# An encoder layer with neighbourhood attention: queries and keys reach their operands by four token tiles instead of by two

## The chip, the core and the metric

The kernel runs on one core of one Trainium2 chip. The metric is the device time in microseconds (us) of one execution. Below, TensorE (PE) is the matrix engine, VectorE (DVE) and ScalarE (ACT) the two engines that read and write both kinds of on-chip memory, GpSimd (POOL) a slower one that cannot reach PSUM, and SyncE (SP) issues all of the DMAs.

## What is computed

One layer is applied to two sequences, a sample of 1024 tokens (8 tiles of 128) and a prompt of 512 tokens (4 tiles). Cut to what matters:

```python
h = rms_norm(x, norm_g)
u_pool, g_pool, q, k, v, g_attn = split(h @ w_in)      # each 512 wide
pool_out = pool_mixer(u_pool, w_pool, pool_scale) * silu(g_pool)
q = rms_norm(q.reshape(B, S, 8, 64), q_norm_g) * 64 ** -0.5
k = rms_norm(k.reshape(B, S, 8, 64), k_norm_g)
attn_out = neighbourhood_attention(q, k, v, rpb) * silu(g_attn)
y = x + concatenate([pool_out, attn_out]) @ w_out
```

The attention sees the tokens as rows of 64 columns; a query sees 8 rows by 16 columns of keys. The 8 heads are worked on in 4 pairs.

## The kernel before, in words

Every matrix product is made of three float32r products, high by high, high by low and low by high, where "low" is what is left of a float32 number after its high part. The helper `split` makes both parts, `low` the second one.

The program goes through the four head pairs of the sample, then through the four of the prompt, then through the output projection (tiles `acco`). For each pair `project_qkv` multiplies a token tile of 128 tokens by 384 columns (queries, keys and values of two heads) into a PSUM bank `acc_s` or `acc_p`: 24 matmuls of 128x384 a tile. For the first pair of the sample four tiles are interleaved; for the others one tile follows another, and the last two are interleaved. Then `gate` and `u_block` make three (prompt) or six (sample) blocks of 24 matmuls of 128x512 (`accg`, `accu`), `attention` makes scores `s`, transposes `pt` and products `po`, and `pooling` the other branch.

What the change touches lies in `project_qkv`. ScalarE copies a finished tile to SBUF (`qkv`, a ring of `QBUFS` = 4 buffers). The squares of its queries and keys (`s2`) are summed per head into `st4`. After two tiles VectorE scales the sums (one `tensor_scalar`) and `rsqrt` takes the reciprocal root of all of them in 11 small instructions. VectorE then multiplies the queries and keys of each tile by these factors, and TensorE transposes them, four 128x128 transposes into one PSUM bank `ptq` (tag `pt`, of which there are two; the attention's transposes take the same tag). From that bank ScalarE writes, for each head of the pair, the keys twice and the queries once (64 partitions by 256), and VectorE writes the low parts of keys and queries. The values go by `vd` in DRAM to the tiles `v`, four loads for two token tiles.

Two engines never work on one PSUM bank at once: the planner makes any access to a bank wait for the accesses that other engines recorded on it before. So in the bank `ptq` all six copies of ScalarE come first, and the four of VectorE after them.

The order on each engine is not the order of the code. Every call is recorded as an operation of `Plan`, with its needs; `Plan.order` then runs a list schedule with costs written by hand and emits the operations in the order that it finds. Matmuls of the projections and blocks have the priority `MAIN` and stay in the order of the program; scores, transposes and attention products have an earlier priority and slip in between as soon as they are ready in the plan. An operation on TensorE counts as ready `TO_PE` = 800 ns after what it needs has ended on another engine. Loading and splitting of weights has the first priority (`FIRST`). On the chip each engine then runs its list strictly in order.

Of the kernel before, what the change touches and what calls it, by code (L numbers as in the profile page):

```python
# [14 lines left out]
F32 = mybir.dt.float32  # L15
# [323 lines left out]
def encoder(ctx, tc, xn_p, xt_p, xn_s, xt_s, w_in, w_out, w_pool, pscale, ng, qg, kg,  # L339
# [26 lines left out]
    qk_t = sb.tile([P, 2], F32, name="qk_t")  # L366
    gqk = sb.tile([P, 1], F32, name="gqk")
# [125 lines left out]
    class Sequence:  # L493
# [63 lines left out]
        def project_qkv(self, p, w, group=1):  # L557
# [3 lines left out]
            for t0 in range(0, self.NT, 2):  # L561
                st4 = ring("st4", 2, [P, 4, 8], f"st4_{sq}_{p}_{t0}")
                qkvs = []
                for t in (t0, t0 + 1):
# [28 lines left out]
                rsqrt(st4[:, 2], st4[:, 3], st4[:, 1])  # L593
                pt = bank("pt", f"ptq_{sq}_{p}_{t0}")
                for i, t in enumerate((t0, t0 + 1)):
                    qkv = qkvs[i]
                    vt = ring("vt", 2, [P, 2, 2, HD], f"vt_{sq}_{p}_{t}", F32R)
                    split(vt[:, :, 0], vt[:, :, 1], qkv[:, 256:384].rearrange("p (h d) -> p h d", d=HD))
                    sp.dma_start(out=vd[t * P:(t + 1) * P, :], in_=vt.rearrange("p h s d -> p (h s d)").bitcast(F32))
                    qn = qkv[:, 0:256].rearrange("p (h d) -> p h d", d=HD)  # L600
                    dve.tensor_tensor(out=qn, in0=qn, op=ALU.mult,
                                      in1=st4[:, 2, i * 4:i * 4 + 4].unsqueeze(2).to_broadcast([P, 4, HD]))
                    pe.transpose(pt[:, i * P:(i + 1) * P], in_=qkv[:, 0:P], identity=ident)
                    pe.transpose(pt[:, 256 + i * P:256 + (i + 1) * P], in_=qkv[:, P:256], identity=ident)
# [4 lines left out]
                rt, r0 = (2 * t0) // 8, (2 * t0) % 8  # L609
                lo, hi = 7 - r0, 3 - r0  # L610
                qa = slice(base + rt * 512, base + (rt + 1) * 512)
                ka = slice(base + t0 * P, base + t0 * P + 256)
                own = [slice(hd * HD, hd * HD + HD) for hd in range(2)]
                k_src = [pt[own[hd], 256:512] for hd in range(2)]
                q_src = [pt[own[hd], 0:256].rearrange("p (r cb c) -> p r cb c", r=4, cb=4) for hd in range(2)]
                q_dst = []
                for hd in range(2):
                    for rows in (own[hd], own[1 - hd]):
                        v = q[hd][rows, qa].rearrange("p (cb r c) -> p r cb c", cb=4, r=8)
                        q_dst.append(v[:, lo::-1, :, ::-1] if hi < 0 else v[:, lo:hi:-1, :, ::-1])  # L620
                for hd in range(2):
                    for rows in (own[hd], own[1 - hd]):
                        act.activation(out=k[hd][rows, ka], in_=k_src[hd], func=AF.Copy, scale=gqk[own[hd]])
                    act.activation(out=q_dst[2 * hd], in_=q_src[hd], func=AF.Copy)
                for hd in range(2):
                    low(k[2 + hd][own[hd], ka], k_src[hd], k[hd][own[hd], ka], gqk[own[hd]])
                    low(q_dst[2 * hd + 1], q_src[hd], q_dst[2 * hd])
                rg = t0 // 2
                for cb in range(4):
                    sa = bass.AP(vd.tensor, vd.offset + (rg * 4 * GW + C0[cb]) * 256,  # L630
                                 [[GW * 256, 4], [256, 32], [1, 256]])
                    sp.dma_start(out=vs[base // 256 + rg][:, cb].bitcast(F32), in_=sa)
# [126 lines left out]
    warm = sb.tile([P, 1], F32, name="warm")  # L759
    dve.memset(warm, 0.0)  # L760
    act.activation(out=warm, in_=warm, func=AF.Exp)
# [312 lines left out]
```

## Time and profile before

| | us |
|---|---|
| median of 3 runs | 648.9 (647.37 to 649.58) |
| the profiled execution | 648.4 |
| its span, first to last instruction | 646.6 |
| TensorE busy in the span | 635.0 |
| VectorE busy in the span | 557.1 |
| ScalarE busy in the span | 372.8 |
| GpSimd busy in the span | 100.6 |

The span is that of one profiled execution; 1.8 us of its time lie outside the span. Busy times are sums of what an engine's instructions took, so a busy TensorE still has to be looked at for how close its matmuls start to each other. The granted TensorE clock is 1.00 throughout.

### The profile page before, as it was taken

The page shows a single profiled execution, that of the slowest core. Times are in us where ns is not written, and L with a number is a line of the kernel's source. Part 1 is how long each engine was busy: PE and PEld are TensorE (multiplying, and loading weights), DVE is VectorE, ACT ScalarE, POOL GpSimd, SP SyncE. Part 2 cuts the span into 40 slices and gives each one's busy share as a digit, 9 for nine tenths or more (in the row PEclk, how much of TensorE's full clock was granted, in tenths as well). Part 3 has the DMA queues.
Part 4 walks back from the last instruction along what each step waited for, and adds up shares of the span by engine and source line. Part 5 has one row for each costly group of instructions (what it writes and reads, how often), then busy time and mean ns, then how long its engine had stood idle before and what let it go on. Part 6 is the DMA issues. An engine that isn't in the chain of part 4 may idle for free.

```text
span 646.6 us, 11390 instructions
## 1 busy us (share of the span) xinstructions
PE 635.0 (98%) x3404; PEld 567.0 (88%) x3404; DVE 557.1 (86%) x1647; ACT 372.8 (58%) x910; POOL 100.6 (16%) x142
## 2 busy tenths in 40 slices
PE   6999999999999999999999999999999999999997
PEld 5998899988899888999889989899899878887886
DVE  6688999899987999967999989989999989879742
ACT  5766786568656476544777556477566457323210
POOL 1130100000000000101001110021212423405412
PEclk9999999999999999999999999999999999999999
DMA  8974354442274522425344355545556687843631
GB/s 304 348 205 143 104 169 124 123 121 79 59 246 137 182 62 69 134 95 152 127 112 143 109 168 162 174 139 144 169 174 195 189 261 231 269 152 118 191 131 65
DMA packets 92961, 101.53 MB, mean 157 GB/s; under 512 B 12900, under 2 KB 78564, under 8 KB 92900
## 3 DMA queue, kind: packets, MB, share of 16 engines
q1 hardware_dynamic: 92900, 100.81, 50.7%
q8 instruction: 27, 0.44, 0.3%
q14 instruction: 34, 0.28, 0.1%
HBM read 81.41 MB, written 19.37 MB: 156 GB/s over the span
## 4 chain that ended last, share of the span: by engine, by line
PE 91%; DVE 4%; DMA 3%; issue 1%; ACT 0%; SPq 0%; DVEq 0%; ACTq 0%
PE acc_s L330 21%; PE acco L330 15%; PE accg_s L330 14%; PE acc_p L330 10%; PE accu_s L330 7%; PE accg_p L330 6%; PE po_s L330 4%; PE accu_p L330 3%; PE pt_s L330 3%; PE s_s L330 3%; DMA xr<-in_xn_s 1%; PE po_p L330 1%; PE ptq_s L330 1%; DVE B L330 1%; PE pt_p L330 1%
## 5 line engine op out<-in xcount | busy, mean ns | idle before, releaser
L330 PE MATMUL acc_s<-w_sA,ht_s 128*128 128x384 f32 x768 | 145.9, 342 | 6.3 <-DVE w_sA L330 6.3
L330 PEld LDWEIGHTS acc_s<-w_sA,ht_s 128*128 128x128 f32 x768 | 136.0, 190 | 7.6 <-ACT ht_s L330 5.9
L330 PE MATMUL accg_s<-ht_s,w_sT 128*128 128x512 f32 x384 | 100.4, 399 | 0.0
L330 PEld LDWEIGHTS accg_s<-ht_s,w_sT 128*128 128x128 f32 x384 | 70.0, 188 | 12.0
L330 PE MATMUL acc_p<-w_pA,ht_p 128*128 128x384 f32 x384 | 75.4, 339 | 0.7 <-DVE w_pA L330 0.5
L330 PEld LDWEIGHTS acc_p<-w_pA,ht_p 128*128 128x128 f32 x384 | 66.1, 188 | 1.8 <-DVE w_pA L330 0.8
L330 PE MATMUL acco<-B,left 128*128 128x512 f32 x228 | 56.2, 395 | 0.6 <-DVE left L330 0.6
L330 PE MATMUL accu_s<-ht_s,w_sT 128*128 128x512 f32 x192 | 53.0, 400 | 0.0
L330 PEld LDWEIGHTS acco<-B,left 128*128 128x128 f32 x228 | 41.9, 188 | 9.5 <-DVE left L330 1.0
L330 PE MATMUL accg_p<-ht_p,w_pT 128*128 128x512 f32 x192 | 47.6, 395 | 0.0
L330 PEld LDWEIGHTS accg_p<-ht_p,w_pT 128*128 128x128 f32 x192 | 35.3, 188 | 6.9
L330 ACT ACTIVATE k<-ptq_s,gqk 64x256 fp32r<-64x256 f32 x64 | 30.1, 470 | 18.8 <-PE ptq_s L330 18.1
L330 PEld LDWEIGHTS accu_s<-ht_s,w_sT 128*128 128x128 f32 x192 | 34.6, 188 | 5.1
L330 DVE TENSOR_TENSOR xr<-acco,xr 128x512 f32<-128x512 f32 x30 | 20.5, 686 | 20.4 <-PE acco L330 18.2
L330 ACT ACTIVATE ns_edge<-ns_edge,sm_s 128x288 f32<-128x288 f32 x54 | 28.4, 529 | 16.5 <-DVE sm_s L330 16.3
L330 ACT ACTIVATE ns_s<-ns_s,sm_s 128x384 f32<-128x384 f32 x53 | 31.7, 610 | 10.1 <-DVE sm_s L330 9.9
L330 DVE TENSOR_TENSOR pp_s<-pt_s,pp_s 128x384 fp32r<-128x384 f32 x64 | 34.5, 544 | 0.3
L330 PE MATMUL po_s<-pp_s,v 128*128 128x256 f32 x192 | 32.0, 287 | 0.0
L330 PE MATMUL s_s<-k,q 128*128 128x288 f32 (+1 forms) x128 | 31.4, 330 | 0.0
L330 PEld LDWEIGHTS po_s<-pp_s,v 128*128 128x128 f32 x192 | 28.9, 188 | 1.5
L330 POOL TENSOR_TENSOR vt_s<-qkv_s,vt_s 128x128 fp32r<-128x128 f32 x17 | 9.1, 540 | 122.0 <-ACT vt_s L330 97.3
L330 ACT ACTIVATE qkv_s<-acc_s,rr_s 128x384 f32<-128x384 f32 x24 | 13.7, 578 | 23.6 <-PE acc_s L330 20.9
(221 smaller groups left out, 1350.4 us busy)
## 6 DMA issues: line engine op xcount, KB each, us to landing
v<-vd_s SPq DMA_DIRECT2D x64, 128.0 KB
wr_sA<-in_w_in SPq DMA_DIRECT2D x32, 192.0 KB
wr_sT<-in_w_in SPq DMA_DIRECT2D x32, 192.0 KB
wr_pA<-in_w_in SPq DMA_DIRECT2D x32, 192.0 KB
wr_pT<-in_w_in SPq DMA_DIRECT2D x32, 192.0 KB
out<-xr SPq DMA_DIRECT2D x24, 256.0 KB
x<-in_xt_s SPq DMA_DIRECT2D x16, 256.0 KB
vd_s<-vt_s SPq DMA_DIRECT2D x32, 128.0 KB
```

The costliest lines, as they stand in the source:

```text
L330: op.fn()
```

## The change

A group of `project_qkv` is now four token tiles, not two. The sample has two groups a pair instead of four, the prompt one instead of two. `st4` holds 16 sums and factors in a row instead of 8, and uses its first part again for the helper values of `rsqrt`. The transposes of the queries go to one bank (`qt`), those of the keys to another (`kt`), both of the tag `pt`. Every copy out of them is 64 partitions by 512. Queries come first, and within a head the low part is recorded right behind its high part. The eight loads of values come behind. The factor `gqk` is now a column of the tile `qk_t`, and the tile `warm` is gone; its first activation works on `gqk`.

```diff
@@ -363,8 +363,8 @@
 
     g_sb = sb.tile([P, KC], F32, name="g_sb")
     ident = sb.tile([P, P], F32, name="ident")
-    qk_t = sb.tile([P, 2], F32, name="qk_t")
-    gqk = sb.tile([P, 1], F32, name="gqk")
+    qk_t = sb.tile([P, 3], F32, name="qk_t")
+    gqk = qk_t[:, 2:3]
     psc = sb.tile([P, NPAIR], F32, name="psc")
     edge = sb.tile([P, NPAIR, 16], F32, name="edge")
 
@@ -558,10 +558,10 @@
             sq, rr, base = self.sq, self.rr, self.base(p)
             accs = {}
             vd = dram.tile([self.S, 256], F32, name=f"vd_{sq}_{p}")
-            for t0 in range(0, self.NT, 2):
-                st4 = ring("st4", 2, [P, 4, 8], f"st4_{sq}_{p}_{t0}")
+            for t0 in range(0, self.NT, 4):
+                st4 = ring("st4", 2, [P, 3, 16], f"st4_{sq}_{p}_{t0}")
                 qkvs = []
-                for t in (t0, t0 + 1):
+                for t in range(t0, t0 + 4):
                     if t not in accs:
 
                         n = group if group > 1 else 2 if t == self.NT - 2 else 1
@@ -590,9 +590,9 @@
                     qkvs.append(qkv)
                 dve.tensor_scalar(out=st4[:, 1], in0=st4[:, 0], scalar1=1.0 / HD, scalar2=EPS,
                                   op0=ALU.mult, op1=ALU.add)
-                rsqrt(st4[:, 2], st4[:, 3], st4[:, 1])
-                pt = bank("pt", f"ptq_{sq}_{p}_{t0}")
-                for i, t in enumerate((t0, t0 + 1)):
+                rsqrt(st4[:, 2], st4[:, 0], st4[:, 1])
+                qt, kt = bank("pt", f"qt_{sq}_{p}_{t0}"), bank("pt", f"kt_{sq}_{p}_{t0}")
+                for i, t in enumerate(range(t0, t0 + 4)):
                     qkv = qkvs[i]
                     vt = ring("vt", 2, [P, 2, 2, HD], f"vt_{sq}_{p}_{t}", F32R)
                     split(vt[:, :, 0], vt[:, :, 1], qkv[:, 256:384].rearrange("p (h d) -> p h d", d=HD))
@@ -600,36 +600,30 @@
                     qn = qkv[:, 0:256].rearrange("p (h d) -> p h d", d=HD)
                     dve.tensor_tensor(out=qn, in0=qn, op=ALU.mult,
                                       in1=st4[:, 2, i * 4:i * 4 + 4].unsqueeze(2).to_broadcast([P, 4, HD]))
-                    pe.transpose(pt[:, i * P:(i + 1) * P], in_=qkv[:, 0:P], identity=ident)
-                    pe.transpose(pt[:, 256 + i * P:256 + (i + 1) * P], in_=qkv[:, P:256], identity=ident)
-
-
-
-
-                rt, r0 = (2 * t0) // 8, (2 * t0) % 8
-                lo, hi = 7 - r0, 3 - r0
-                qa = slice(base + rt * 512, base + (rt + 1) * 512)
-                ka = slice(base + t0 * P, base + t0 * P + 256)
+                    pe.transpose(qt[:, i * P:(i + 1) * P], in_=qkv[:, 0:P], identity=ident)
+                    pe.transpose(kt[:, i * P:(i + 1) * P], in_=qkv[:, P:256], identity=ident)
+
+
+
+
+                qa = slice(base + t0 * P, base + (t0 + 4) * P)
                 own = [slice(hd * HD, hd * HD + HD) for hd in range(2)]
-                k_src = [pt[own[hd], 256:512] for hd in range(2)]
-                q_src = [pt[own[hd], 0:256].rearrange("p (r cb c) -> p r cb c", r=4, cb=4) for hd in range(2)]
-                q_dst = []
+                k_src = [kt[own[hd]] for hd in range(2)]
+                q_src = [qt[own[hd]].rearrange("p (r cb c) -> p r cb c", r=8, cb=4) for hd in range(2)]
+                q_dst = [q[hd][rows, qa].rearrange("p (cb r c) -> p r cb c", cb=4, r=8)[:, ::-1, :, ::-1]
+                         for hd in range(2) for rows in (own[hd], own[1 - hd])]
+                for hd in range(2):
+                    act.activation(out=q_dst[2 * hd], in_=q_src[hd], func=AF.Copy)
+                    low(q_dst[2 * hd + 1], q_src[hd], q_dst[2 * hd])
                 for hd in range(2):
                     for rows in (own[hd], own[1 - hd]):
-                        v = q[hd][rows, qa].rearrange("p (cb r c) -> p r cb c", cb=4, r=8)
-                        q_dst.append(v[:, lo::-1, :, ::-1] if hi < 0 else v[:, lo:hi:-1, :, ::-1])
-                for hd in range(2):
-                    for rows in (own[hd], own[1 - hd]):
-                        act.activation(out=k[hd][rows, ka], in_=k_src[hd], func=AF.Copy, scale=gqk[own[hd]])
-                    act.activation(out=q_dst[2 * hd], in_=q_src[hd], func=AF.Copy)
-                for hd in range(2):
-                    low(k[2 + hd][own[hd], ka], k_src[hd], k[hd][own[hd], ka], gqk[own[hd]])
-                    low(q_dst[2 * hd + 1], q_src[hd], q_dst[2 * hd])
-                rg = t0 // 2
-                for cb in range(4):
-                    sa = bass.AP(vd.tensor, vd.offset + (rg * 4 * GW + C0[cb]) * 256,
-                                 [[GW * 256, 4], [256, 32], [1, 256]])
-                    sp.dma_start(out=vs[base // 256 + rg][:, cb].bitcast(F32), in_=sa)
+                        act.activation(out=k[hd][rows, qa], in_=k_src[hd], func=AF.Copy, scale=gqk[own[hd]])
+                    low(k[2 + hd][own[hd], qa], k_src[hd], k[hd][own[hd], qa], gqk[own[hd]])
+                for rg in range(t0 // 2, t0 // 2 + 2):
+                    for cb in range(4):
+                        sa = bass.AP(vd.tensor, vd.offset + (rg * 4 * GW + C0[cb]) * 256,
+                                     [[GW * 256, 4], [256, 32], [1, 256]])
+                        sp.dma_start(out=vs[base // 256 + rg][:, cb].bitcast(F32), in_=sa)
 
 
         def gate(self, p, w, out, col, b):
@@ -756,9 +750,8 @@
     ss, pr = Sequence("s", 1024, 12, hts_s, Rb_s), Sequence("p", 512, 8, hts_p, Rb_p)
 
 
-    warm = sb.tile([P, 1], F32, name="warm")
-    dve.memset(warm, 0.0)
-    act.activation(out=warm, in_=warm, func=AF.Exp)
+    dve.memset(gqk, 0.0)
+    act.activation(out=gqk, in_=gqk, func=AF.Exp)
     sp.dma_start(out=g_sb, in_=ng)
     w = []
     for b in range(2):
```

What the planner makes of it is shown at three places. In the names `acc_s_3_702` is the projection of token tile 3 of the sample, `ptq_s_0` the old bank of the group that begins at tile 0, `qt_s_0` and `kt_s_0` the new ones; `k_..` and `q_..` are operands of the attention; a number at the end only tells buffers apart.

First TensorE, in the projection of the sample's fourth pair. Before:

```order
L330 MATMUL acc_s_3_702<-w_sA_2_676,ht_s_0_108 128x384 x3
L330 MATMUL acc_s_3_702<-w_sA_3_678,ht_s_0_109 128x384 x2
L330 MATMUL ptq_s_0_695<-ident,qkv_s_0_690 128x128 x2
L330 MATMUL ptq_s_0_695<-ident,qkv_s_1_693 128x128 x2
L330 MATMUL acc_s_3_702<-w_sA_3_678,ht_s_0_109 128x384
```

Now:

```order
L330 MATMUL acc_s_5_703<-w_sA_1_666,ht_s_1_114 128x384 x3
L330 MATMUL acc_s_5_703<-w_sA_2_668,ht_s_1_115 128x384 x2
L330 MATMUL qt_s_0_693<-ident,qkv_s_0_682 128x128
L330 MATMUL kt_s_0_694<-ident,qkv_s_0_682 128x128
L330 MATMUL acc_s_5_703<-w_sA_2_668,ht_s_1_115 128x384
L330 MATMUL qt_s_0_693<-ident,qkv_s_1_685 128x128
L330 MATMUL kt_s_0_694<-ident,qkv_s_1_685 128x128
L330 MATMUL acc_s_5_703<-w_sA_3_670,ht_s_1_116 128x384
```

The first transposes stood 11 matmuls into `acc_s_3`, with the 24 of `acc_s_2` between them and tile 1, the last of their group. They now stand 8 matmuls into `acc_s_5`, with the 24 of `acc_s_4` between them and tile 3, the last of the new group, and come in lots of two.

Next ScalarE at the same place, with what each row waits for. Before:

```order
L330 ACTIVATE k_94<-ptq_s_0_695,gqk 64x256 [waits PE_49]
L330 ACTIVATE k_94<-ptq_s_0_695,gqk 64x256
L330 ACTIVATE q_92<-ptq_s_0_695 64x4x4x16
L330 ACTIVATE k_95<-ptq_s_0_695,gqk 64x256 x2
L330 ACTIVATE q_93<-ptq_s_0_695 64x4x4x16
L330 ACTIVATE qkv_s_3_703<-acc_s_3_702,rr_s 128x384 [waits PE_49]
```

Now:

```order
L330 ACTIVATE qkv_s_4_701<-acc_s_4_700,rr_s 128x384 [waits DVE_49,PE_49,Pool_49]
L330 ACTIVATE s_s_4_702<-qkv_s_4_701 128x256 [waits Activation_49]
L330 ACTIVATE q_91<-qt_s_0_693 64x8x4x16 [waits PE_49]
L330 ACTIVATE k_93<-kt_s_0_694,qk_t 64x512 [waits PE_49]
L330 ACTIVATE k_93<-kt_s_0_694,qk_t 64x512
L330 ACTIVATE q_92<-qt_s_0_693 64x8x4x16 [waits DVE_49]
L330 ACTIVATE qkv_s_5_704<-acc_s_5_703,rr_s 128x384 [waits PE_49,Pool_49]
L330 ACTIVATE k_94<-kt_s_0_694,qk_t 64x512 [waits DVE_49]
L330 ACTIVATE k_94<-kt_s_0_694,qk_t 64x512
```

Six copies of one bank in a row, to which VectorE's four were the sequel, have become six of twice the size from two banks, and two of them wait for VectorE's low parts, which now run between them.

Last TensorE at the end of the prompt's fourth pair, where the output projection (`acco`) begins. Before:

```order
L330 MATMUL accm_p_0_1280<-ph,wpl_p_1275 128x512
L330 MATMUL acco_1_1350<-B_2_1303,left_1296 128x512
L330 MATMUL ptq_p_2_1208<-ident,qkv_p_2_1204 128x128 x2
L330 MATMUL acco_1_1350<-B_2_1303,left_1296 128x512
L330 MATMUL acco_1_1350<-B_3_1304,left_1296 128x512 x3
L330 MATMUL acco_1_1353<-B_0_1281,a_0_0_1337 128x512 x3
```

Now:

```order
L330 MATMUL accg_p_0_256_1259<-ht_p_127,w_pT_6_1210 128x512 x3
L330 MATMUL accg_p_0_256_1259<-ht_p_128,w_pT_7_1212 128x512 x3
L330 MATMUL s_p_0_2_1225<-k_93,q_91 128x256
L330 MATMUL s_p_0_2_1225<-k_95,q_91 128x256
L330 MATMUL s_p_0_3_1231<-k_93,q_91 128x192
L330 MATMUL s_p_0_3_1231<-k_95,q_91 128x192
L330 MATMUL acco_1_1335<-B_0_1267,left_1279 128x512 x3
```

The last transposes of queries and keys (`ptq_p_2`) stood among the first 60 matmuls of the output projection, and the scores `s_p` behind them. The transposes now stand in `accu_p`, ahead of these rows, and four of the eight lots of scores of the pair ahead of the first `acco`.

## Rows read from the trace of the kernel before

**Rows 1.** The page, busy time of each engine (share of the span) and instructions.

```profile
PE 635.0 (98%) x3404; PEld 567.0 (88%) x3404; DVE 557.1 (86%) x1647; ACT 372.8 (58%) x910; POOL 100.6 (16%) x142
```

**Rows 2.** The page, chain of work that ended last, by engine.

```profile
PE 91%; DVE 4%; DMA 3%; issue 1%; ACT 0%; SPq 0%; DVEq 0%; ACTq 0%
```

**Rows 3.** Busy time by stretch: length, PE, PEld, DVE, ACT, POOL, clock, DMA share, GB/s.

```profile
370.00:470.00 100.00, 100.00 (x545) 89.67 (x544) 93.13 (x296) 60.60 (x155) 17.26 (x28) 1.00 0.53 160
470.00:511.00 41.00, 40.28 (x223) 36.20 (x222) 39.26 (x126) 26.03 (x71) 9.78 (x12) 1.00 0.61 182
511.00:550.00 39.00, 38.72 (x194) 31.60 (x193) 35.07 (x103) 25.09 (x70) 13.21 (x19) 1.00 0.77 239
550.00:640.00 90.00, 89.44 (x391) 72.78 (x390) 63.11 (x117) 22.90 (x54) 30.58 (x28) 1.00 0.49 160
sum 600.00, PE 598.44 PEld 531.69 DVE 529.01 ACT 346.40 POOL 92.44; mean PE 74.81 PEld 66.46 DVE 66.13 ACT 43.30 POOL 11.55
```

**Rows 4.** Waits of PE: line, released by: us in total, times, longest.

```profile
PE acc_s L330 <- DVE w_sA L330: 6.3, 2, 5.9
PE acc_p L330 <- DVE w_pA L330: 0.5, 1, 0.5
```

**Rows 5.** The chain in order of time: start, length, work; two unbroken pieces of TensorE.

```profile
282.87 9.37 PE acc_s L330 x53
302.46 5.50 PE accg_s L330 x24
```

**Rows 6.** Timeline of DVE from 455 us: start, length, instruction; two rows of it.

```profile
473.24 0.48 DVE L330 SCALAR_TENSOR_TENSOR k<-ptq_p,gqk,k 64x256 fp32r<-64x256 f32 x1
473.64 0.54 DVE L330 TENSOR_TENSOR w_pA<-wr_pA,w_pA 128x384 fp32r<-128x384 f32 x1
```

**Rows 7.** Groups by line and form, small instructions: count | busy us, mean ns | idle before.

```profile
L330 DVE SCALAR_TENSOR_TENSOR st_s<-st_s 128x8 f32<-128x8 f32 x96 | 16.6, 174 | 2.0
L330 DVE TENSOR_TENSOR st_s<-st_s 128x8 f32<-128x8 f32 x48 | 8.1, 169 | 0.9
L330 DVE TENSOR_SCALAR st_s<-st_s 128x8 int32<-128x8 int32 x32 | 5.4, 168 | 0.7
```

**Rows 8.** The same view: four copies from `ptq`, and three of 512 columns from PSUM.

```profile
L330 ACT ACTIVATE k<-ptq_s,gqk 64x256 fp32r<-64x256 f32 x64 | 30.1, 470 | 18.8 <-PE ptq_s L330 18.1
L330 ACT ACTIVATE q<-ptq_s 64x256 fp32r<-64x256 f32 x32 | 12.1, 379 | 0.4
L330 DVE SCALAR_TENSOR_TENSOR k<-ptq_s,gqk,k 64x256 fp32r<-64x256 f32 x32 | 15.4, 483 | 8.1 <-ACT q L330 7.6
L330 DVE TENSOR_TENSOR q<-ptq_s,q 64x256 fp32r<-64x256 f32 x32 | 13.5, 422 | 0.6
L330 DVE TENSOR_TENSOR xr<-acco,xr 128x512 f32<-128x512 f32 x30 | 20.5, 686 | 20.4 <-PE acco L330 18.2 <-POOL xr L330 1.2 <-DMA xr<-in_xn_s 1.0
L330 ACT ACTIVATE p<-acco 128x512 f32<-128x512 f32 x4 | 2.4, 594 | 13.1 <-PE acco L330 13.1
L330 DVE SCALAR_TENSOR_TENSOR sgp<-accm_s,psc,sgp 128x512 f32<-128x512 f32 x8 | 5.9, 743 | 1.0 <-PE accm_s L330 0.9
```

**Rows 9.** Timelines of ACT, DVE and PE, the sample's fourth pair, tile 1 to its transposes.

```profile
275.66 0.58 ACT L330 ACTIVATE qkv_s<-acc_s,rr_s 128x384 f32<-128x384 f32 x1 [3.43 <-PE acc_s L330]
...
277.54 0.68 DVE L330 TENSOR_TENSOR ph<-tree_s,ph 128x512 fp32r<-128x512 f32 x1
...
279.85 0.75 DVE L330 SCALAR_TENSOR_TENSOR sgp<-accm_s,psc,sgp 128x512 f32<-128x512 f32 x1
...
280.91 0.76 DVE L330 TENSOR_TENSOR qkv_s<-qkv_s,st_s 128x256 f32<-128x256 f32 x2
...
282.27 0.60 PE L330 MATMUL ptq_s<-ident,qkv_s 128*128 128x128 f32 x4
```

**Rows 10.** Busy time of ten us, columns as in rows 3.

```profile
520.00:530.00 10.00, 9.85 (x47) 7.69 (x46) 7.86 (x20) 5.55 (x15) 1.79 (x3) 1.00 0.87 284
```

**Rows 11.** DMA issues: out<-in, queue, count, KB each.

```profile
rT<-in_w_out SPq DMA_DIRECT2D x32, 128.0 KB
```

## The prediction

> **What bounds the kernel now.** I read the page first: busy times, then the chain that ended last. TensorE is busy for 635.0 of 646.6 us [rows 1] and makes up 91% of the chain [rows 2]. The reader should distrust a busy TensorE, because a matmul's record overlaps the next one's. So I looked at how close matmuls start. In unbroken pieces of the chain 53 matmuls of 128x384 take 9.37 us, 0.177 each, and 24 of 128x512 take 5.50 us, 0.229 each [rows 5]. The stretches show the same count of matmuls per time in the sample and in the prompt, and no idle time of note: from 40 to 640 us TensorE is idle for 1.56 us in all, 0.72 of it between 470 and 511, 0.28 between 511 and 550 and 0.56 between 550 and 640 [rows 3]. The rest of the idle time is the 6.3 us for the first weights [rows 4] and the last additions and stores, which the change does not touch. So whatever other engines save, the middle of the program can give back about 1.6 us, 0.24% of 648.4. A measurement of this kernel can tell some 0.3% from no change, about 1.9 us.
>
> **The change, part by part.** The counts of matmuls and transposes stay: 3404 records on TensorE, in another order. What shrinks is work of VectorE and ScalarE.
>
> Small instructions. A group has 12 of them, one scaling and 11 in the root. There were 16 groups in the sample and 8 in the prompt. The sample's cost 16.6 + 8.1 + 5.4 us and half of the last again for the plain `tensor_scalar` forms, 2.7, so 32.8 us for 192 [rows 7]; with half as many in the prompt 49 us. Half of the groups go: 24.6 us less busy time, less some 8 ns for 8 more columns on the 144 that stay, so about 23 us of VectorE.
>
> Low parts. 48 of keys at 483 ns and 48 of queries at 422 become 24 and 24 of twice the size. The nearest rows with 512 columns from PSUM have 743 ns (with a scale from a column) and 686 [rows 8]. That is 43.4 us before and 34.3 after: 9 us saved.
>
> Copies on ScalarE. 96 of keys at 470 and 48 of queries at 379 ns become 48 and 24. A 512-column copy from PSUM without a scale took 594, and the scale added 91 at 256 columns, so I take 594 and 685 [rows 8]: 63.3 us become 47.1, 16 us saved.
>
> All of it lies beside TensorE's stream, so I cost it at nothing, with one exception. TensorE's wait for `w_pA` near 473 us ends behind a queue of VectorE in which the low part of the keys stands right before the split that TensorE waits for [rows 6]. The wait is put down to VectorE, 0.5 us [rows 4], and the stretch lost 0.72 [rows 3]. Around such a place VectorE now has 8 low parts of about 0.45 less 4 of about 0.71, 0.8 us, and 12 small instructions of 0.17, 2.0 us, less to do. I take the 0.72 as gone. The idle time after 511 us I keep, since it lies behind other work there: loads at 284 GB/s with the DMA engines 87% busy [rows 10], and additions of the output projection. What is late next, were VectorE faster still, is TensorE itself.
>
> The added waits. Two copies on ScalarE now wait for VectorE's low part in the middle of a group. Behind them on ScalarE stands the copy of tile 5 out of its bank; the block `accg` needs that bank only after the 48 matmuls of tiles 6 and 7, 8.5 us at 0.177. The copy of tile 4 now waits for the first transposes, because all four `qkv` buffers are taken by one group. Tile 7's first matmul needs its bank: 19 matmuls and 6 transposes later, over 3.4 us, for one copy of 0.58 [rows 9]. Both hold. The scores start later, by some 3 to 4 us a pair; TensorE has blocks to do meanwhile.
>
> The moved DMAs. Eight loads of values now come behind a group, and near the output projection the four `rT` loads, freed by the earlier transposes, come ahead of the second lot of `B` weights on SP. Four times 128 KB [rows 11] at 284 GB/s [rows 10] are 1.8 us. The bounds are 0 and 1.8; I take 0, because the value loads of this place have moved behind some of those weights.
>
> The sum, from the profiled execution: 648.4 - 0.7 = 647.7. The median of the shown runs lies 0.5 above that execution, which would make 648.2. I say 648.0.
>
> A rule speaks against this sum. The Trainium skill, "Perfetto Trace Analysis", Identifying the Most-Contended Engine, says that matmul busy time does not tell the distance to the peak and that the busy share of weight loads does. By it TensorE is 88% full, not 98% [rows 1]. The trace answers with start distances: the shares differ because a 128x512 matmul takes longer than the load of its weights, so that this rule finds room where the matmuls leave none.
>
> **The rivals.** First, TensorE does keep pace with VectorE in hidden small gaps, and relief of VectorE shortens whole stretches. For it: VectorE is busy 93.1 of 100 and 39.3 of 41 us in the prompt [rows 3]. There it would save a third of 32 us, 10.7, and if a quarter of that came through with all 1.56 us of idle time, the time would be 648.4 - 2.7 - 1.6, about 644. Against it are the equal start distances. Near it lies the plain good case: all the idle time goes, 646.8.
>
> Second, slower: TensorE runs into the transposes before the factors are ready. It works in order, so it stops there, with all projection matmuls behind it. In the sample's fourth pair the chain from the copy of tile 1 to the scaled queries ran from 275.66 to 281.67 with two other works of 0.68 and 0.75 in it, and the transposes started at 282.27, 0.6 us later [rows 9]. Free of these the chain is 4.6 us. In the new order there are 32 matmuls, 5.7 us, between tile 3's end and the transposes; the copy begins some 0.3 us after that end, so 0.8 us of slack are left, and nothing stands within the chain there. In the prompt 26 to 34 matmuls of 0.229 stand in between, 6.0 us at least; but two tiles end together, so a second copy of 0.58 comes into the chain: 5.2 us and 0.3 of start, 0.5 of slack. Where more than that slips in between, TensorE waits. There are 10 such groups outside the sample's first pair, two in each of its three others and one in each pair of the prompt. If each were late by 0.4 us, it would cost 4.0 and the time would be 648.4 + 4.0 = 652.4. For it: VectorE is 93 to 96% busy in the prompt, and in the last pair splits of `B` stand within the small instructions. Against it: 24 groups ran with the same sort of slack before, and the waits of TensorE name none of them.
>
> The Trainium skill has a rule on this side too ("Perfetto Trace Analysis", Optimizing Scalar/DVE Operations): larger operations help an engine that is saturated, and where an engine is not but makes others wait, smaller ones let work end sooner. ScalarE at 58% [rows 1] is of the second kind. By that rule the change goes the wrong way, and the late case just priced is what it would give.
>
> Third, the loads at the start of the output projection are late by the full 1.8 us: 649.8.
>
> **How the numbers follow.** My forecast, a small gain or none: 0.55, at 648.0, from 647.2 to 649.0. Late loads, 649.8: 0.08, within 0.3%. The plain good case at 646.8: 0.12, of which about half is measured as over 0.3%. The relief of whole stretches, 644: 0.05. Late transposes, 650 to 653: 0.20, nearly all of it beyond 650.8, where 0.3% above the median begins. So faster 0.06 + 0.05, with 0.01 for the low end of the forecast, 0.12; slower 0.20; the rest, 0.68, within 0.3%. The range reaches from 646.6 to 652.4 and leaves out the relief case and the far part of the late one.
>
> **What would show it.** Right: VectorE near 525 us busy, ScalarE near 357, TensorE still near 635, and no wait of TensorE for `w_pA` near 473. Copies near 685 and 594 ns, low parts near 743 and 686. Wrong: waits of TensorE for `qkv` or `st4` at `qt`, or a gap between the last `accg_p` and the first `acco`; on the other side, 128x384 matmuls that start less than 0.175 us apart.

## The result, and the profile after

The changed kernel takes 652.6 us (median of 4 runs, 652.12 to 653.4) where the kernel before takes 648.6 (4 runs, 647.37 to 649.58). The ratio is 1.0064, with an interval from 1.0043 to 1.0085: slower by some 4 us, clear of the 0.3% that a measurement can tell from no change. The forecast was 648.0, and the range of the text ended at 652.4. The profiled execution took 652.3, its span 650.5.

The page of the changed kernel, its row of busy times, answers to [rows 1]:

```profile
PE 639.0 (98%) x3404; PEld 566.8 (87%) x3404; DVE 537.3 (83%) x1473; ACT 352.2 (54%) x829; POOL 94.0 (14%) x133
```

Every other engine has less to do, as the change meant. TensorE has the same 3404 instructions and is busy 4.0 us longer, and that is the whole loss. The stretches, with the columns of [rows 3], show that it doesn't stand idle for it:

```profile
40.00:470.00 430.00, 429.60 (x2403) 388.20 (x2402) 372.70 (x1084) 253.75 (x596) 31.65 (x53) 1.00 0.45 132
470.00:511.00 41.00, 40.68 (x226) 36.28 (x226) 37.84 (x116) 25.97 (x68) 6.59 (x10) 1.00 0.64 189
511.00:550.00 39.00, 38.67 (x189) 31.50 (x188) 33.84 (x94) 22.25 (x67) 14.62 (x18) 1.00 0.74 226
550.00:640.00 90.00, 89.43 (x387) 72.09 (x386) 64.00 (x116) 23.51 (x56) 31.86 (x31) 1.00 0.52 166
```

From 470 us on the idle time is 1.22 us, where it was 1.56. Before 470 us 0.40 us have come in, where there was none, so that the sum from 40 to 640 us is 1.62: what was saved behind 470 us was lost ahead of it. In the last 90 us, where TensorE has little but the output projection left, it starts 387 instructions instead of 391, at the same granted clock of 1.00. The same matmuls go by more slowly. Two unbroken pieces of the chain say it for one form at a time (start, length, work, as in [rows 5]):

```profile
303.93 5.61 PE accg_s L330 x24
447.17 7.46 PE acc_p L330 x43
```

The same block `accg_s` of the sample's fourth pair took 5.50 us before: 24 matmuls of 128x512 have gone from 229 to 234 ns each. Those of 128x384, on the other hand, are a little faster: 43 in 7.46 us are 173.5 ns, where [rows 5] had 177 (over the whole trace the difference is smaller, 173.9 against 175.1, as the table below shows). I took the distance from each matmul's start to the next over the whole trace: the 128x512 groups of projection and output sum up to 334.1 us (330.0 before), the 128x384 ones to 207.1 (208.2), all the rest to 99.5 (98.4). That is 4.1, -1.1 and 1.1 us.

The waits of TensorE (in total, times, longest; compare [rows 4]) hold a part of the rest:

```profile
PE acc_s L330 <- DVE w_sA L330: 6.1, 2, 5.7
PE acco L330 <- DVE left L330: 0.6, 1, 0.6
PE po_p L330 <- DVE sm_p L330: 0.3, 1, 0.3
PE qt_p L330 <- DVE qkv_p L330: 0.3, 1, 0.3
PE qt_s L330 <- DVE qkv_s L330: 0.2, 1, 0.2
```

The wait for `w_pA` near 473 us is gone. Two new ones stand at the transposes `qt`, 0.5 us together, and a third of 0.3 at the products `po_p`.

### The profile page after: what moved, and what is told of

It reads as the page before. It is cut to its first block, busy times and chain, and to the rows that moved or that the text cites. A ratio compares the mean times of both kernels' runs of the same rounds, so it can differ in the third digit from the quotient of the medians.

```text
span 650.5 us, 11103 instructions
## 1 busy us (share of the span) xinstructions
PE 639.0 (98%) x3404; PEld 566.8 (87%) x3404; DVE 537.3 (83%) x1473; ACT 352.2 (54%) x829; POOL 94.0 (14%) x133
## 4 chain that ended last, share of the span: by engine, by line
PE 81%; DMA 9%; DVE 6%; issue 2%; ACT 1%; SPq 0%; POOL 0%; DVEq 0%; POOLq 0%; ACTq 0%
PE acco L330 16%; PE acc_s L330 16%; PE accg_s L330 11%; PE acc_p L330 10%; PE accu_s L330 7%; PE accg_p L330 5%; PE po_s L330 3%; PE pt_s L330 3%; DMA rB<-in_w_out 3%; PE s_s L330 3%; PE accu_p L330 3%; DMA xh_p<-in_xn_p 2%; DMA wpool_s<-in_w_pool 1%; PE po_p L330 1%; DMA wr_sT<-in_w_in 1%
## 5 line engine op out<-in xcount | busy, mean ns | idle before, releaser
L330 PE MATMUL acc_s<-w_sA,ht_s 128*128 128x384 f32 x768 | 144.2, 343 | 6.1 <-DVE w_sA L330 6.1
L330 PE MATMUL accg_s<-ht_s,w_sT 128*128 128x512 f32 x384 | 102.4, 401 | 0.0
L330 PE MATMUL acco<-B,left 128*128 128x512 f32 x228 | 54.8, 393 | 0.6 <-DVE left L330 0.6
L330 ACT ACTIVATE ns_s<-ns_s,sm_s 128x384 f32<-128x384 f32 x56 | 33.9, 610 | 13.5 <-DVE sm_s L330 13.3
L330 ACT ACTIVATE ze<-ze 128x512 f32<-128x512 f32 x24 | 15.1, 629 | 29.3 <-DVE ze L330 28.2
L330 DVE TENSOR_TENSOR pv_s<-po_s,pv_s 64x256 f32<-64x256 f32 x64 | 26.2, 409 | 0.9 <-ACT pv_s L330 0.8
```

The costliest lines, as they stand in the source:

```text
L330: op.fn()
```

## The experiments

**The theories.** Three were put on trial. *Order*: the new order of the work, with its later transposes, costs the 4 us. *Places*: the change also moves tiles in SBUF, and TensorE's pace depends on where its two operands begin. *The forecast's own*: the change saves TensorE about 0.7 us, and something that the forecast didn't look at hides that.

The places come straight out of the diff. Each allocation takes a multiple of 32 bytes in a partition. Between the tiles `ht` (16 of 4096 bytes) and the weights stood, before, `rr_s` 32, `ss_s` 64, `rr_p` 32, `ss_p` 32 and `warm` 32: 192 bytes. Without `warm` they are 160. The tiles `ht`, the weights, the staging buffers between them and the slices that a matmul takes of them are multiples of 256 bytes long, so that this distance, modulo 256, holds for every matmul of `ht` with a weight. A 128x512 matmul streams `ht` (or `left`) and holds the weight; a 128x384 matmul streams the weight and holds `ht`, so for it the distance is 256 minus that. The tiles of `acco` lie in the same two places: `left` and a part of `B` both take old buffers of `ht`, at a distance of 0 in every kernel, which makes these matmuls a control.

**First, the old kernel with moved tiles.** One line goes up, and nothing else changes, in no engine's order.

```diff
     edge = sb.tile([P, NPAIR, 16], F32, name="edge")
+    warm = sb.tile([P, 1], F32, name="warm")
...
-    warm = sb.tile([P, 1], F32, name="warm")
```

> The kernel before, with one line moved: the 4-byte tile warm is allocated ahead of the large tiles, so that ht, k, q, v, B and left begin 32 bytes later in each partition, as they nearly do in the changed kernel; weights stay where they were, and every engine's order is the same. Theory of places (TensorE's pace depends on where its operands begin): 128x512 matmuls of accg_s start 233 to 234 ns apart instead of 229.9, those of 128x384 173.6 instead of 175.2, and the time is 652 to 653. Theory of order (the new order of the work costs the 4 us): nothing changes, 648.6.

Measured: 651.91 us, ratio 1.0057 [1.0040, 1.0075]. Most of the loss is there without the change. Timeline of TensorE in four kernels, each with the same two blocks: 24 `accg_s` of the sample's fourth pair, and the 96 `acco` of the control (start, length). Before:

```profile
302.30 5.67 PE L330 MATMUL accg_s<-ht_s,w_sT 128*128 128x512 f32 x24
562.05 22.09 PE L330 MATMUL acco<-B,left 128*128 128x512 f32 x96
```

The changed kernel:

```profile
303.76 5.77 PE L330 MATMUL accg_s<-ht_s,w_sT 128*128 128x512 f32 x24
565.23 22.05 PE L330 MATMUL acco<-B,left 128*128 128x512 f32 x96
```

The kernel before with `warm` moved up:

```profile
304.52 5.77 PE L330 MATMUL accg_s<-ht_s,w_sT 128*128 128x512 f32 x24
566.35 22.13 PE L330 MATMUL acco<-B,left 128*128 128x512 f32 x96
```

The block with the new distance takes 0.10 us more in both, 4 ns a matmul; the control, whose two operands were moved together, takes what it took. The order theory has no answer to the third pair of rows.

**The changed kernel with `ht` put back.** `rr_s` is allocated ahead of the large tiles, which puts `ht` on a boundary of 64 bytes again.

```diff
+    rr_s = sb.tile([P, 8], F32, name="rr_s")
...
-            self.rr = sb.tile([P, self.NT], F32, name=f"rr_{sq}")
+            self.rr = rr_s if sq == "s" else sb.tile([P, self.NT], F32, name=f"rr_{sq}")
```

> The changed kernel, with the 32-byte tile rr_s allocated ahead of the large tiles, so that ht, k, q, v, B and left begin on the addresses of the kernel before; weights and order are untouched. Theory of places: 128x512 matmuls of accg_s 229 to 230 ns apart, 128x384 near 175, TensorE busy near 635, time 647.5 to 648.8, which is what the change itself is worth. Theory of order: 652.6 as the changed kernel, pace as there (233.6 ns).

Measured: 651.23 us, 1.0038 [1.0023, 1.0052]. The expectation was missed: 128x512 matmuls start 232.3 ns apart, not 229 to 230. A boundary of 64 bytes under `ht` is not what counts, and I had to look at both operands.

**The changed kernel with the weights moved down by 32 bytes** (`rr_s` allocated behind the weights):

```diff
+            if sq == "p":
                 self.rr = sb.tile([P, self.NT], F32, name=f"rr_{sq}")
...
     w_t = load_w(w_in[1], BW, "sT0")
+    ss.rr = sb.tile([P, 8], F32, name="rr_s")
```

> The changed kernel, with the 32-byte tile rr_s allocated behind the weights, so that the weights begin 32 bytes earlier; ht and the rest stay off a 64-byte boundary, where the change put them, and now the weights are off it too. If what counts is that both operands of a matmul lie alike: 128x512 at 228.6 ns, as the acco matmuls of left and B have in the changed kernel where both begin 32 bytes off, and a time of 647 to 649. If what counts is that the moving operand itself is off a 64-byte boundary: 128x512 stay at 233.6, 128x384 become slower too (178 to 180), time 654 to 658. Theory of order: 652.6.

Measured: 651.87 us, 1.0053 [1.0036, 1.0069], 128x512 at 232.4 ns and 128x384 at 176.0. Neither form of the expectation held. But these two runs agree with each other to 0.1 ns, one with all on 64-byte boundaries and one with none: what they share is that `ht` and weights are 128 apart.

**The kernel before with a gap of 64 bytes**, which makes the distance 0:

```diff
     ss, pr = Sequence("s", 1024, 12, hts_s, Rb_s), Sequence("p", 512, 8, hts_p, Rb_p)
+    gap = sb.tile([P, 16], F32, name="gap")
```

> The kernel before, with an unused gap of 64 bytes ahead of the weights: ht and the weights now both begin on a multiple of 256 bytes, where they were 192 bytes apart modulo 256. Order untouched. By the acco matmuls of the kernel before (227.8 ns where both lie alike modulo 512, 229.0 to 231 elsewhere) the 128x512 matmuls might gain 1 to 2 ns, 1300 of them 1 to 2.5 us: 646 to 648. If only 64 bytes count, nothing changes: 648.6 and 229.9 ns. Theory of order: 648.6.

Measured: 647.27 us, 0.9973 [0.9959, 0.9986], in the expected range and below the kernel before: 128x384 went from 175.1 to 174.2 ns, 128x512 from 229.8 to 229.5. The time came as expected, but most of the gain stands at the 128x384 matmuls and not, as the expectation had it, at the 128x512.

**Both orders on the same places.** The next runs part the change from its side effect. First, the old order on the changed kernel's addresses:

```diff
-    qk_t = sb.tile([P, 2], F32, name="qk_t")
-    gqk = sb.tile([P, 1], F32, name="gqk")
+    qk_t = sb.tile([P, 3], F32, name="qk_t")
+    gqk = qk_t[:, 2:3]
...
-    warm = sb.tile([P, 1], F32, name="warm")
-    dve.memset(warm, 0.0)
-    act.activation(out=warm, in_=warm, func=AF.Exp)
+    dve.memset(gqk, 0.0)
+    act.activation(out=gqk, in_=gqk, func=AF.Exp)
...
     w_t = load_w(w_in[1], BW, "sT0")
+    gap = sb.tile([P, 32], F32, name="gap")
```

> The kernel before, order untouched, with every large tile on the address that it has in the changed kernel (gqk becomes a column of qk_t and takes over the warming activation, an unused gap of 128 bytes stands behind the weights). The runs so far say that the start distance of matmuls goes by how far apart their two operands begin modulo 256 bytes: here, as in the changed kernel, 160 for the 128x512 of ht and weights, so 233.6 ns, and 128x384 near 174. Theory of places, the change itself worth nothing: 652 to 653, as the changed kernel. Theory that the change itself saves the 0.7 forecast: 653. Theory that the change itself costs: 650 to 651.5, with the rest of the 4 us due to the order.

Measured: 651.31 us, 1.0048 [1.0036, 1.0060]. The pace is that of the changed kernel (233.5 and 174.0 ns), so most of the loss is there in the old order too. The time lies 0.7 us below the range of the theory of places and inside the one set for a change that itself costs something; the pair at the end of this section decides that. Then the new order with a distance of 0 (the four small tiles go ahead of the large ones), and the old order on these places (there with the edits just shown as well):

```diff
+    rr_s = sb.tile([P, 8], F32, name="rr_s")
+    ss_s = sb.tile([P, 2, 8], F32, name="ss_s")
+    rr_p = sb.tile([P, 4], F32, name="rr_p")
+    ss_p = sb.tile([P, 2, 4], F32, name="ss_p")
...
-            self.rr = sb.tile([P, self.NT], F32, name=f"rr_{sq}")
-            self.ss = sb.tile([P, 2, self.NT], F32, name=f"ss_{sq}")
+            self.rr = rr_s if sq == "s" else rr_p
+            self.ss = ss_s if sq == "s" else ss_p
```

> The changed kernel, with the four small tiles rr_s, ss_s, rr_p and ss_p (160 bytes) allocated ahead of the large ones: ht and weights, 160 bytes apart modulo 256, come to 0 apart (both at 128). Order untouched. Theory of the distance between operands: 128x512 of ht and weights from 233.6 to 228.5 to 230, some 1100 of them, 4 to 5 us less; 128x384 stay near 174: 648. If the absolute boundary counted, both at 128 could differ from both at 0. Theory of order: 652.6.

> The kernel before with the same small tiles moved, so that all large tiles lie as in the changed kernel with both operands at 128. It is the partner of that kernel: the ratio of the two is what the change itself is worth on equal and good places. Theory of places, change worth nothing: equal, both 647 to 648. By my forecast the changed kernel is 0.7 lower. If late transposes cost something, the changed kernel is 0.5 to 2 us higher.

Measured: the new order 645.95 us, 0.9962 [0.9951, 0.9974]; the old order 646.84, 0.9980 [0.9969, 0.9991]. The changed kernel gained 6.7 us by 160 bytes of small tiles, and is ahead of both kernels; the 648 expected was too high by 2 us. Start distances account for some 4.5 us of the gain (4.1 ns on about 1100 matmuls of 128x512), and idle time of TensorE from 40 to 640 us for 0.6 (0.98 where it was 1.62). Where the rest comes from is not shown. Its timeline, the same two blocks as above:

```profile
301.45 5.64 PE L330 MATMUL accg_s<-ht_s,w_sT 128*128 128x512 f32 x24
559.97 22.02 PE L330 MATMUL acco<-B,left 128*128 128x512 f32 x96
```

and its waits of TensorE, where those at `qt` are missing too:

```profile
PE acc_s L330 <- DVE w_sA L330: 6.8, 2, 6.4
PE acco L330 <- DVE left L330: 0.6, 1, 0.6
PE po_p L330 <- DVE sm_p L330: 0.4, 1, 0.4
```

**A fifth distance.** Only `rr_s` and `ss_s` go ahead:

```diff
+    rr_s = sb.tile([P, 8], F32, name="rr_s")
+    ss_s = sb.tile([P, 2, 8], F32, name="ss_s")
...
+            self.rr = rr_s if sq == "s" else sb.tile([P, self.NT], F32, name=f"rr_{sq}")
+            self.ss = ss_s if sq == "s" else sb.tile([P, 2, self.NT], F32, name=f"ss_{sq}")
```

> The changed kernel, with rr_s and ss_s (96 bytes) allocated ahead of the large tiles: ht begins at 64, weights at 128 modulo 256; 64 apart for the 128x512 (192 for the 128x384). Order untouched. The few acco matmuls with 64 between their operands start 231 ns apart; by them 128x512 gain 2.6 ns of 233.6, some 1100 of them, 2.9 us; no row shows 128x384 at 192: 649 to 651. Theory that only a 64-byte boundary counts: as where all lie at multiples of 64, 229 to 232.

Measured: 650.26 us, 1.0031 [1.0018, 1.0044], 128x512 at 233.0 and 128x384 at 173.5. All are at multiples of 64, and the pace is bad for the one form (231 was expected) and the best of all for the other. Boundaries are out. This run has a late group of transposes as well, in the sample's first pair:

```profile
PE qt_s L330 <- DVE more L330: 1.3, 1, 1.3
PE po_s L330 <- DVE pp_s L330: 0.8, 1, 0.8
```

The start distances of all these kernels, as means over the matmuls that follow one of their own kind (some 690 of 128x512 with `ht`, some 1025 of 128x384, some 200 of the control), side by side. The few per cent that lie far above the rest are left out (about 40 of 128x512, at 313 to 322 ns, in the kernel before). The last column compares to about half a microsecond, since the kernel before itself took 648.1 to 648.9 us beside the other runs:

| kernel | order | apart for 128x512 | ns | apart for 128x384 | ns | control, ns | us |
|---|---|---|---|---|---|---|---|
| before | old | 192 | 229.8 | 64 | 175.1 | 228.2 | 648.6 |
| `warm` moved | old | 160 | 233.6 | 96 | 174.2 | 228.5 | 651.9 |
| on the new places | old | 160 | 233.5 | 96 | 174.0 | 228.7 | 651.3 |
| changed | new | 160 | 233.6 | 96 | 173.9 | 228.9 | 652.6 |
| `ht` put back | new | 128 | 232.3 | 128 | 175.9 | 228.5 | 651.2 |
| weights down | new | 128 | 232.4 | 128 | 176.0 | 228.9 | 651.9 |
| 64 apart | new | 64 | 233.0 | 192 | 173.5 | 228.3 | 650.3 |
| gap of 64 | old | 0 | 229.5 | 0 | 174.2 | 227.9 | 647.3 |
| 0 apart | old | 0 | 229.4 | 0 | 174.2 | 228.1 | 646.8 |
| 0 apart | new | 0 | 229.5 | 0 | 174.0 | 228.2 | 646.0 |

Rows with one distance agree to 0.3 ns, whatever the order and wherever both operands begin. The 0 of `gap of 64` is 256 bytes of small tiles, that of the last two rows is none at all: 256 bytes more make no difference.

**TensorE alone.** Is it the other engines, which read and write the same memory, that make one distance slow? One program runs nothing but rows of 48 matmuls on one tile:

```diff
+    def series(bank, n, apart, count=48, shift=0, every=None):
+        with plan.priority(MAIN):
+            for i in range(count):
+                m = shift // 4 + 512 * (i % 2)
+                gap = every[i % len(every)] if every else apart
+                s = 1024 + shift // 4 + gap // 4 + 128 * (i % 4)
+                pe.matmul(bank[:, 0:n], lhsT=src[:, s:s + P], rhs=src[:, m:m + n],
+                          start=i % 24 == 0, stop=i % 24 == 23)
```

> Leaves out the whole computation: TensorE alone runs rows of 48 matmuls on zeros from one tile, in which the stationary operand begins 0, 32, ... 224 bytes (modulo 256) behind the moving one (banks a to h in this order), for 512 and for 384 columns, each twice; then a few with both operands moved by 32 or 96 bytes, then rows in which 0 and 160 alternate, and last four of the distances again while VectorE and ScalarE copy without a pause. If the distance alone sets the pace, it shows here without any other engine at work: 512 columns 228 to 229 ns apart at 0, 232 at 32, 233 at 64, 232 at 128, 233.6 at 160, 229.6 at 192, and the same with both operands moved; 384 columns 174 at 0, 176 at 128, 173.5 at 192. If the pace comes from other engines that read and write the same memory, all rows without them are alike, near 213 plus a constant for 512, and differ only at the end.

Its timeline of TensorE (start, length; `bank_a` is 0 apart, `bank_b` 32, and so on to `bank_h` 224; the rows at 350 and 373 us with both operands moved, by 32 and 96; from 414 us on with VectorE adding and ScalarE copying):

```profile
37.74 11.35 PE L330 MATMUL bank_b<-src 128*128 128x512 f32 x48
48.93 11.36 PE L330 MATMUL bank_c<-src 128*128 128x512 f32 x48
60.13 11.40 PE L330 MATMUL bank_d<-src 128*128 128x512 f32 x48
71.37 11.32 PE L330 MATMUL bank_e<-src 128*128 128x512 f32 x48
82.53 11.37 PE L330 MATMUL bank_f<-src 128*128 128x512 f32 x48
93.73 11.16 PE L330 MATMUL bank_g<-src 128*128 128x512 f32 x48
104.72 11.36 PE L330 MATMUL bank_h<-src 128*128 128x512 f32 x48
...
115.92 8.51 PE L330 MATMUL bank_a<-src 128*128 128x384 f32 x48
140.97 8.64 PE L330 MATMUL bank_d<-src 128*128 128x384 f32 x48
149.45 8.61 PE L330 MATMUL bank_e<-src 128*128 128x384 f32 x48
166.38 8.48 PE L330 MATMUL bank_g<-src 128*128 128x384 f32 x48
...
261.64 11.37 PE L330 MATMUL bank_g<-src 128*128 128x512 f32 x48
350.66 22.57 PE L330 MATMUL bank_f<-src 128*128 128x512 f32 x96
373.07 11.07 PE L330 MATMUL bank_a<-src 128*128 128x512 f32 x48
414.75 11.05 PE L330 MATMUL bank_a<-src 128*128 128x512 f32 x48
448.03 11.35 PE L330 MATMUL bank_f<-src 128*128 128x512 f32 x48
```

With 512 columns a row takes 11.05 to 11.07 us at a distance of 0 and 11.32 to 11.40 at every other one but 192, that is 227 ns from start to start against 232.5 to 234; moving both operands changes nothing, and two busy engines change nothing. So the loss needs no other engine at work. In this program each distance has a PSUM bank of its own, so that it alone could not part the two; in the kernels above the edits left every matmul's PSUM bank as it was, and the pace went with the distance. Two things don't fit a rule by the distance alone. At 192 one row took 11.16 us and another, in the same bank, 11.37. And 384 columns at 96 start 176.6 ns apart here, 174 in the kernels. Something else counts too, which these runs don't tell.

**Is the change itself worth something?** Once more the changed kernel and its partner on the same places, with no new edit, one after the other on one chip:

> The changed kernel as it is, once more, on the same chip as the next one, so that the two can be divided. 652 to 652.8 by its first result.

> The kernel before on the addresses of the changed kernel, once more, as the partner of the run ahead. If the change itself is worth the same at 160 bytes as at 0 (0.9 us less): it comes out 0.9 above the changed kernel, 652.5 to 653.5. If waits at the new transposes, which the changed kernel has three of at 160 bytes and none at 0, give the gain back: equal or up to 1 us below it, 651 to 652.5.

Measured: 652.84 us, 1.0061 [1.0046, 1.0076], and 652.52, 1.0054 [1.0037, 1.0071]. At 160 apart the two orders, 0.3 us from each other, can't be told apart, so the order does not make the loss; nor does the gain of 0.9 us show here that the two orders had at a distance of 0. The partner, too, has waits in its profiled execution there that the kernel before has not:

```profile
PE s_p L330 <- DVE q L330: 1.3, 1, 1.3
PE pt_s L330 <- ACT ns_edge L330: 0.6, 1, 0.6
```

Last, the changed kernel at a distance of 0 again, in another session:

> The changed kernel with both operands at 128 modulo 256 once more, on another chip or at another time, since its first five times lay within 0.2 us of each other and its partner's within 3. If the 645.95 is what these addresses give: 645.5 to 646.6, ratio to the kernel before 0.995 to 0.997, no wait of TensorE at qt. If it was luck: 646.8 to 648, as its partner.

Measured: 646.04 us, 0.9973 [0.9961, 0.9985]. The gain against the changed kernel stands; the narrow spread of its first five runs was luck (now 644.84 to 648.4). Against its partner's 646.84 it is 0.8 to 0.9 us less, with intervals that overlap. One part of the expectation was missed: the execution profiled this time has the wait in the prompt again, so that its absence above belongs to that one execution.

```profile
PE qt_p L330 <- DVE qkv_p L330: 0.3, 1, 0.3
```

## Why the prediction was wrong, point by point

**The step that failed** stands at the head of the part on the change: the counts of matmuls and transposes stay, so TensorE's work stays at 635 us. The start distances of 0.177 and 0.229 us [rows 5] were carried over as if they belonged to the shapes. They belong to the shapes and to the places of the operands. The lines that decided it were in the diff and were costed at nothing without a look: `gqk` becomes a column, `warm` goes. By the table, 3.8 ns more on the 864 matmuls of 128x512 of the projections and some 230 of the output projection are 4.2 us, and 1.2 less on 1152 of 128x384 are 1.4: 2.8 us. The old order on the new places lost 3.2 and 3.8 us in its two comparisons (651.31 against 648.11, 652.52 against 648.72), and 3.0 with `warm` moved (651.91 against 648.87). That term was missing, and no rival had it. These three comparisons leave 0.2 to 1.0 of the 4.0 us in the result unexplained, and the runs can't tell that much from nothing.

One reading on the way was loose as well: the count of matmuls per time is not quite the same in the sample and in the prompt of the kernel before (515 in the 90 us from 40 us on, 5.7 a us; 545 in the 100 us from 370 us on, 5.45). The start distances of one form agree there (230.2 ns for `accg_s`, 229.8 for `accg_p`), and the argument needs no more than that.

The prediction had named 128x384 matmuls less than 0.175 us apart as a sign that relief of VectorE reaches TensorE. They came (173.9 ns), but the old order on the new places has them as well (174.0): here they are a sign of the places.

**The other steps.** The wait for `w_pA` went as forecast: every execution of the old order has it, between 472 and 478 us, and none of the new order does. But the 0.7 us were not kept in the changed kernel, whose idle time from 40 to 640 us is 1.62 us against 1.56, with the waits at `qt` among the new ones. That the rest of the relief is worth nothing agrees with the runs: on equal places the change gives 0.8 to 0.9 us at a distance of 0, which is not clear of the noise, and nothing that can be measured at 160.

The busy times: VectorE fell by 19.8 us and not by 32, ScalarE by 20.6 where I had 16, GpSimd by 6.6. The durations were right. The groups after, by line and form (columns as in [rows 7]; [rows 8] had 470, 379, 483 and 422 ns for half the columns):

```profile
L330 ACT ACTIVATE k<-kt_s,qk_t 64x512 fp32r<-64x512 f32 x32 | 21.8, 681 | 1.4 <-DVE k L330 1.1
L330 ACT ACTIVATE q<-qt_s 64x512 fp32r<-64x512 f32 x16 | 9.5, 591 | 10.5 <-PE qt_s L330 9.2 <-DVE q L330 1.1
L330 DVE SCALAR_TENSOR_TENSOR k<-kt_s,qk_t,k 64x512 fp32r<-64x512 f32 x16 | 12.0, 750 | 3.9 <-ACT k L330 3.6
L330 DVE TENSOR_TENSOR q<-qt_s,q 64x512 fp32r<-64x512 f32 x16 | 11.0, 689 | 3.6 <-ACT q L330 3.2
L330 DVE SCALAR_TENSOR_TENSOR st_s<-st_s 128x16 f32<-128x16 f32 x48 | 8.4, 174 | 1.3
L330 DVE TENSOR_TENSOR st_s<-st_s 128x16 f32<-128x16 f32 x24 | 4.6, 191 | 0.7
```

I had taken 685, 594, 743 and 686 ns. What was off is the count. The change takes 144 small instructions and 48 low parts from VectorE and 72 copies from ScalarE; the page shows 174, 81 and 9 fewer on the three engines. The planner let the relieved VectorE take over 18 others from its neighbours.

**The rival of late transposes** was right in its place and small in its price. Two of the ten groups were late, one of them in the prompt's last pair, as its text named it. Timeline of VectorE there (start, length), with splits of `B` within the chain of small instructions and a multiplication of the gate (`ze`) behind it:

```profile
500.08 0.29 DVE L330 CAST B<-rB 128x256 fp32r<-128x256 f32 x1
500.28 0.17 DVE L330 SCALAR_TENSOR_TENSOR st_p<-st_p 128x16 f32<-128x16 f32 x1
500.40 0.43 DVE L330 TENSOR_TENSOR B<-rB,B 128x256 fp32r<-128x256 f32 x1
...
502.75 0.68 DVE L330 TENSOR_TENSOR ze<-accg_p,Rb_s 128x512 f32<-128x512 f32 x1
503.35 0.75 DVE L330 TENSOR_TENSOR qkv_p<-qkv_p,st_p 128x256 f32<-128x256 f32 x2
```

and of TensorE, which stood for it (in brackets what it waited for):

```profile
503.91 0.30 PE L330 MATMUL qt_p<-ident,qkv_p 128*128 128x128 f32 x1 [0.28 <-DVE qkv_p L330]
```

The other late group, at 226 us, cost 0.24. The sample's first pair, which the rival left out, was late by 0.4 to 1.3 us in four of the new order's seven profiled executions, and in none of the two at a distance of 0. So the mechanism is real, and the waits at `qt` come to at most 1.5 us in one execution (64 apart), not four; that its 652.4 in the text lies near the measured time is chance. The two rules of the Trainium skill that the prediction set against the trace ("Perfetto Trace Analysis") don't explain the loss either: the smaller operations that Optimizing Scalar/DVE Operations suggests could have spared at most these waits, 0.5 us at `qt` in the changed kernel, and no run tried them; the busy share of weight loads, by which TensorE had room, went from 88% to 87% while TensorE set the time. **The loads** of the output projection were not late: no wait of TensorE for `B` is listed.

## What to carry to other kernels

An edit that adds, drops or resizes a small tile moves every tile behind it; before its effect is put down to the work it changes, compare the start distances of matmuls that it does not touch, and run the old order on the new addresses. Where TensorE is the bound and its matmuls start at an even pace, that pace is itself a number to tune: here a few small tiles allocated earlier were worth 6.7 us, and the change under study at most 0.9, which is not clear of the noise.

## What the runs showed of the hardware that was not expected

In these kernels the start distance of back-to-back matmuls, each with its own weight load, went with how far apart the moving (streamed) and the stationary (held) operand begin in a partition, modulo 256 bytes. For 128x512: 229.5 ns at 0, 229.8 at 192, 232.3 at 128, 233.0 at 64, 233.6 at 160; for 128x384: 173.5 at 192, 174 at 0 and 96, 175.1 at 64, 176 at 128. With TensorE alone the spread for 512 columns is 227 to 234 ns, and the distance is not the whole rule there: 192 gave 229 in one row and 233 in another.

The Trainium skill, "SBUF — State Buffer", Who interferes with whom, lists two read ports of TensorE, one for the moving operand and one for weight loads, as independent, and has only the port pair that VectorE and GpSimd share contend. By it the rows of one form would be alike when TensorE runs alone. Here they are not: 11.05 us at a distance of 0 and 11.35 at 160 for 48 matmuls of one form. The measurement decides on the time; whether the two reads disturb each other, and where, no run shows, and it stays open.
